# Weighted expert combine on one core: a ring of token slots with one load queue in place of four two-token buffers on two queues

## The chip, the cores and the metric

The kernel runs on one core of a Trainium2 chip. The metric is device time in microseconds (us) of one launch. The kernel before was timed in four runs: 721.25 to 721.85 us, median 721.6 us. One further view of it exists, a profiled execution of 721.47 us, and every duration below comes from that one.

## The reference: what is computed

```python
batch, seq, n_experts, expert_dim = 16, 1024, 8, 512      # all float32
def reference(expert_outputs, combine_weights):
    weights = combine_weights[..., np.newaxis]
    return np.sum(expert_outputs * weights, axis=2).astype(np.float32)
```

For each of 16,384 tokens, eight rows of 512 numbers are multiplied by eight scalars and added up. The input is 268.4 MB, the output 33.6 MB, the weights 0.5 MB. There is no reuse: each input number is read once, multiplied once and added once.

## The kernel before, in words

**Tiling.** 128 partitions each take J = 2 tokens that follow each other, so that one step holds 256 tokens and there are 64 steps. A step's input tile `in_t` is 32 KiB on each partition (4 MiB in all), and the 128 pieces follow each other in memory without a gap. In what follows a "token" is one row of 128 tokens, one on each partition; a step is then two tokens, and the kernel has 128 of them.

**Loads.** `issue_load` (L52 to L62) allots one of four `in_t` buffers and one of four small `w_t` buffers. The 4 MiB load goes to SyncE's queue (SP) for even steps and to ScalarE's (ACT) for odd steps (L56); the last two steps are loaded in two halves (L59). The weights of a step, 8 KiB, are loaded through GpSimd's queue (L60). Three loads are issued ahead; at step n the load of step n+3 is issued, into the buffer that step n-1 has used. So it waits until VectorE has finished step n-1.

**Arithmetic.** For each of the two tokens in turn, VectorE (DVE) writes the product with expert 0 into `acc` (L77, a TENSOR_SCALAR), then seven times adds a product on top (L83, a SCALAR_TENSOR_TENSOR that reads `in_t`, the scalar and `acc`, and writes `acc`). Each of these seven depends on the one before it.

**Stores.** After each step 512 KiB go out (L92), on the queue that did not load that step; each partition's piece is 4 KiB. Loads and stores thus stand behind each other in both queues.

**The last two steps** (L94 on). Experts 4 to 7 of each token are multiplied on ScalarE into bf16 (L111), while VectorE does experts 0 to 3 (L116, L122), sums the products (L130, L135) and adds them (L138). Four stores of 256 KiB on SP end the kernel (L141).

The order of instructions on each queue is that of the program; the framework adds the semaphore waits.

Of the kernel before, what the change touches and what calls it, by code (L numbers as in the profile page):

```python
# [1 line left out]

# [4 lines left out]


@with_exitstack  # L10
def kernel(
    ctx: ExitStack,
    tc: tile.TileContext,
    expert_outputs: bass.AP,
    combine_weights: bass.AP,
    out: bass.AP,
):
    nc = tc.nc
    fp32 = mybir.dt.float32
    bf16 = mybir.dt.bfloat16  # L20

    B, S, E, D = expert_outputs.shape
    T = B * S
    P = 128
    J = 2
    n_steps = T // (P * J)

    eo_blk = expert_outputs.rearrange("b s e d -> (b s) e d").rearrange(
        "(n p j) e d -> n p j e d", p=P, j=J
    )  # L30
    w_blk = combine_weights.rearrange("b s e -> (b s) e").rearrange(
        "(n p j) e -> n p j e", p=P, j=J
    )
    o_blk = out.rearrange("b s d -> (b s) d").rearrange(
        "(n p j) d -> n p j d", p=P, j=J
    )

    in_pool = ctx.enter_context(tc.tile_pool(name="in_pool", bufs=4))
    w_pool = ctx.enter_context(tc.tile_pool(name="w_pool", bufs=4))
    out_pool = ctx.enter_context(tc.tile_pool(name="out_pool", bufs=4))  # L40
    prod_pool = ctx.enter_context(tc.tile_pool(name="prod_pool", bufs=2))

    ES = E // 2
    K_TAIL = 2

    load_engines = [nc.sync, nc.scalar]

    LA = 3
    in_tiles: list[bass.AP | None] = [None] * n_steps
    w_tiles: list[bass.AP | None] = [None] * n_steps  # L50

    def issue_load(m: int) -> None:  # L52
        in_t = in_pool.tile([P, J, E, D], fp32, name="in_t")
        w_t = w_pool.tile([P, J, E], fp32, name="w_t")
        if m < n_steps - K_TAIL:
            load_engines[m % 2].dma_start(out=in_t, in_=eo_blk[m])  # L56
        else:
            for j in range(J):
                load_engines[m % 2].dma_start(out=in_t[:, j], in_=eo_blk[m, :, j])  # L59
        nc.gpsimd.dma_start(out=w_t, in_=w_blk[m])  # L60
        in_tiles[m] = in_t
        w_tiles[m] = w_t  # L62

    for m in range(min(LA, n_steps)):
        issue_load(m)

    for n in range(n_steps):
        if n + LA < n_steps:
            issue_load(n + LA)
        if n >= n_steps - K_TAIL:  # L70
            continue
        in_tile = in_tiles[n]
        w_tile = w_tiles[n]
        acc = out_pool.tile([P, J, D], fp32)

        for j in range(J):
            nc.vector.tensor_scalar_mul(  # L77
                out=acc[:, j, :],
                in0=in_tile[:, j, 0, :],
                scalar1=w_tile[:, j, 0:1],  # L80
            )
            for e in range(1, E):
                nc.vector.scalar_tensor_tensor(  # L83
                    out=acc[:, j, :],
                    in0=in_tile[:, j, e, :],
                    scalar=w_tile[:, j, e : e + 1],
                    in1=acc[:, j, :],
                    op0=mybir.AluOpType.mult,
                    op1=mybir.AluOpType.add,
                )  # L90

        load_engines[(n + 1) % 2].dma_start(out=o_blk[n], in_=acc)  # L92

    tail_steps = list(range(n_steps - K_TAIL, n_steps))  # L94
    tail_accs = {}
    tail_prods = {}
    for n in tail_steps:
        acc = out_pool.tile([P, J, D], fp32, name="acc")
        prods = prod_pool.tile([P, J, E - ES, D], bf16, name="prods")
        tail_accs[n] = acc  # L100
        tail_prods[n] = prods

    for j in range(J):
        for n in tail_steps:
            in_tile = in_tiles[n]
            w_tile = w_tiles[n]
            acc = tail_accs[n]
            prods = tail_prods[n]

            for e in range(ES, E):  # L110
                nc.scalar.mul(  # L111
                    out=prods[:, j, e - ES, :],
                    in_=in_tile[:, j, e, :],
                    mul=w_tile[:, j, e : e + 1],
                )
            nc.vector.tensor_scalar_mul(  # L116
                out=acc[:, j, :],
                in0=in_tile[:, j, 0, :],
                scalar1=w_tile[:, j, 0:1],
            )  # L120
            for e in range(1, ES):
                nc.vector.scalar_tensor_tensor(  # L122
                    out=acc[:, j, :],
                    in0=in_tile[:, j, e, :],
                    scalar=w_tile[:, j, e : e + 1],
                    in1=acc[:, j, :],
                    op0=mybir.AluOpType.mult,
                    op1=mybir.AluOpType.add,
                )
            nc.vector.tensor_add(  # L130
                out=prods[:, j, 0:2, :],
                in0=prods[:, j, 0:2, :],
                in1=prods[:, j, 2:4, :],
            )
            nc.vector.tensor_add(  # L135
                out=prods[:, j, 0, :], in0=prods[:, j, 0, :], in1=prods[:, j, 1, :]
            )
            nc.vector.tensor_add(  # L138
                out=acc[:, j, :], in0=acc[:, j, :], in1=prods[:, j, 0, :]
            )  # L140
            nc.sync.dma_start(out=o_blk[n, :, j], in_=acc[:, j, :])  # L141


# [1 line left out]
_INS = ['expert_outputs', 'combine_weights']  # L145
_OUTS = [((16, 1024, 512), 'float32')]


# [23 lines left out]
```

## Time and profile before

| What | Value |
|---|---|
| median of four runs | 721.6 us |
| the profiled execution | 721.47 us |
| its span in the profile | 719.7 us |
| outside the span | 1.8 us |
| VectorE busy | 644.3 us (90%), 1020 instructions |
| ScalarE busy | 11.4 us, 17 instructions |
| GpSimd busy | 35.6 us, 68 instructions |
| bytes read from and written to memory | 268.96 MB and 33.55 MB |
| first VectorE instruction starts at | 22.86 us |
| last VectorE instruction ends at | 716.08 us |

The span is the stretch from the first to the last recorded event. "Busy" is the union of an engine's instructions; two VectorE instructions that follow each other overlap a little in these records, so that the mean length of one (744 ns for L83) is more than the distance from one start to the next. The DMA rows count the core's 16 DMA engines together: a share of 100% is all 16 moving a packet. The queue of SP is q1, that of ACT is q10, GpSimd's is q0, and q14 fetches instructions.

### The profile page before, as it was taken

To read this page: it belongs to the slowest core of one execution; us is meant where nothing else is said; L and a number is where in the kernel's file an instruction comes from. 1 tells how busy PE (TensorE), PEld (TensorE's weight loads), DVE (VectorE), ACT (ScalarE), POOL (GpSimd) and SP (SyncE) were. 2 spreads that over 40 slices of the span, in tenths; PEclk is the share of its full clock that TensorE was granted. 3 is DMA by queue.
4 is the path that set the end of the run, shared out by engine and by line. 5 is a ranking of instruction groups with operands and counts; after the bars stand their busy time and mean duration, and the time that the engine had idled before them with its cause. 6 is when DMAs were issued, how large, how long until landed. Compare 5 with 4: busy or idle time off the path is not lost.

```text
span 719.7 us, 1532 instructions
## 1 busy us (share of the span) xinstructions
DVE 644.3 (90%) x1020; ACT 11.4 (2%) x17; POOL 35.6 (5%) x68
## 2 busy tenths in 40 slices
DVE  0799999999998999989998999989998999999977
ACT  0000000000000000000000000000000000000023
POOL 1000000000000000000000000000000000000000
DMA  9999999999999999999999999999999999999983
GB/s 380 438 413 446 434 427 430 428 423 428 442 431 441 427 424 427 428 431 438 437 435 426 431 427 428 434 441 431 430 429 427 424 434 439 435 428 429 424 356 138
DMA packets 21068, 302.63 MB, mean 420 GB/s; under 512 B 3136, under 2 KB 4160, under 8 KB 12608
## 3 DMA queue, kind: packets, MB, share of 16 engines
q1 hardware_dynamic: 9792, 151.52, 49.2%
q10 hardware_dynamic: 9216, 150.47, 48.9%
q0 software_dynamic: 2048, 0.53, 0.3%
q14 instruction: 12, 0.10, 0.0%
HBM read 268.96 MB, written 33.55 MB: 420 GB/s over the span
## 4 chain that ended last, share of the span: by engine, by line
DMA 64%; DVE 35%; issue 1%; DVEq 0%; SPq 0%
DMA out_dram<-acc 56%; DVE acc L83 30%; DMA in_t<-in_expert_outputs_dram 8%; DVE acc L77 3%; DVE acc L122 1%; DVE acc L138 0%; DVE prods L130 0%; DVE acc L116 0%; DVE prods L135 0%; DVEq L77 0%; DVEq L116 0%; SPq L92 0%
## 5 line engine op out<-in xcount | busy, mean ns | idle before, releaser
L83 DVE SCALAR_TENSOR_TENSOR acc<-in_t,w_t,acc 128x512 f32<-128x512 f32 x868 | 580.1, 744 | 0.0
L77 DVE TENSOR_SCALAR acc<-in_t,w_t 128x512 f32<-128x512 f32 x124 | 54.6, 482 | 66.2 <-DMA in_t<-in_expert_outputs_dram 43.3
L60 POOL DMA_DIRECT2D w_t<-in_combine_weights_dram x64 | 35.4, 554 | 637.8 <-DVE acc L83 637.0
L111 ACT ACT_TABLE_LOAD x1 | 1.3, 1283 | 690.5 <-DMA in_t<-in_expert_outputs_dram 690.5
L111 ACT ACTIVATE prods<-in_t,w_t 128x512 bf16<-128x512 f32 x16 | 10.1, 710 | 9.2 <-DMA in_t<-in_expert_outputs_dram 9.1
L122 DVE SCALAR_TENSOR_TENSOR acc<-in_t,w_t,acc 128x512 f32<-128x512 f32 x12 | 8.8, 742 | 0.0
L116 DVE TENSOR_SCALAR acc<-in_t,w_t 128x512 f32<-128x512 f32 x4 | 1.9, 479 | 5.5 <-DMA out_dram<-acc 5.5
L138 DVE TENSOR_TENSOR acc<-acc,prods 128x512 f32<-128x512 f32 x4 | 2.7, 684 | 0.0
L130 DVE TENSOR_TENSOR prods<-prods 128x1024 bf16<-128x1024 bf16 x4 | 2.7, 681 | 0.0
L135 DVE TENSOR_TENSOR prods<-prods 128x512 bf16<-128x512 bf16 x4 | 1.7, 413 | 0.0
L156 POOL MEMSET const-float32-0.0<- 128x1 f32 x1 | 0.1, 98 | 0.2 <-issue 0.2
L156 POOL MEMSET const-bfloat16-1.0<- 128x1 bf16 x1 | 0.1, 102 | 0.0
L156 POOL MEMSET const-float32-1.0<- 128x1 f32 x1 | 0.1, 98 | 0.0
L156 POOL MEMSET const-uint8-127<- 128x1 uint8 x1 | 0.1, 98 | 0.0
## 6 DMA issues: line engine op xcount, KB each, us to landing
in_t<-in_expert_outputs_dram ACTq DMA_DIRECT2D x31, 4096.0 KB, 33.5
in_t<-in_expert_outputs_dram SPq DMA_DIRECT2D x31, 4096.0 KB, 33.3
out_dram<-acc ACTq DMA_DIRECT2D x31, 512.0 KB, 33.5
out_dram<-acc SPq DMA_DIRECT2D x31, 512.0 KB, 33.4
in_t<-in_expert_outputs_dram SPq DMA_DIRECT2D x2, 2048.0 KB, 31.2
in_t<-in_expert_outputs_dram ACTq DMA_DIRECT2D x2, 2048.0 KB, 14.0
w_t<-in_combine_weights_dram POOLq DMA_DIRECT2D x64, 8.0 KB, 6.8
out_dram<-acc SPq DMA_DIRECT2D x4, 256.0 KB, 2.6
```

The costliest lines, as they stand in the source:

```text
L60: nc.gpsimd.dma_start(out=w_t, in_=w_blk[m])
L77: nc.vector.tensor_scalar_mul(out=acc[:, j, :], in0=in_tile[:, j, 0, :], scalar1=w_tile[:, j, 0:1],)
L83: nc.vector.scalar_tensor_tensor(out=acc[:, j, :], in0=in_tile[:, j, e, :], scalar=w_tile[:, j, e : e + 1], in1=acc[:, j, :], op0=mybir.Al ...
L111: nc.scalar.mul(out=prods[:, j, e - ES, :], in_=in_tile[:, j, e, :], mul=w_tile[:, j, e : e + 1],)
L116: nc.vector.tensor_scalar_mul(out=acc[:, j, :], in0=in_tile[:, j, 0, :], scalar1=w_tile[:, j, 0:1],)
L122: nc.vector.scalar_tensor_tensor(out=acc[:, j, :], in0=in_tile[:, j, e, :], scalar=w_tile[:, j, e : e + 1], in1=acc[:, j, :], op0=mybir.Al ...
L130: nc.vector.tensor_add(out=prods[:, j, 0:2, :], in0=prods[:, j, 0:2, :], in1=prods[:, j, 2:4, :],)
L135: nc.vector.tensor_add(out=prods[:, j, 0, :], in0=prods[:, j, 0, :], in1=prods[:, j, 1, :])
L138: nc.vector.tensor_add(out=acc[:, j, :], in0=acc[:, j, :], in1=prods[:, j, 0, :])
L156: nc = _bacc.Bacc("TRN2", target_bir_lowering=False, num_devices=1)
```

## The change

The change rewrites the function.

- **Token blocks.** A block is G = 8 tokens that follow each other on each partition, and there are 16 blocks. On one partition a block is 128 KiB of input that lies together, and the next partition's begins 128 KiB further on.
- **Ring.** In place of four two-token buffers there is one tile, `ring`, of ten slots of one token each (16 KiB on a partition). Loads take two slots, 4 MiB, a pair of tokens. The 32 KiB on each partition lie together in memory, and the next partition's 32 KiB are 128 KiB further on; they were adjacent before.
- **One load queue.** All loads go to SP. Four are issued at once, the fifth next; then the load of tokens i+8 and i+9 is issued after VectorE has finished tokens i-2 and i-1, whose slots it takes.
- **Weights.** All weights go into one tile by one DMA on SP ahead of the first load, as 2048 pieces of 256 bytes. The 64 loads through GpSimd's queue are gone.
- **First product.** `first` moves the product with expert 0 to ScalarE, for all 128 tokens. It writes f32 into `acc`, one pair ahead of VectorE.
- **Two chains in turn.** VectorE does experts 1 to 7 of two tokens alternately: token i expert 1, token i+1 expert 1, token i expert 2, and so on. `acc` has sixteen rows, two blocks.
- **Stores.** A block's eight tokens go out in one DMA of 2 MiB on ACT's queue (16 KiB on a partition). The last block goes out as four tokens on ACT, two on SP, and one and one on SP.
- **End.** The last two tokens are loaded in six pieces (experts 0 to 3 and 4 to 7 of token 126; then 3, 2, 2 and 1 experts of token 127). The split between VectorE and ScalarE in the last two steps, and its bf16 products, are gone.
- `PE_TOKENS` is 0, so the branch with TensorE never runs; `make_identity` still fills a tile on GpSimd at the start.

The diff, cut to its core:

```diff
-    in_pool = ctx.enter_context(tc.tile_pool(name="in_pool", bufs=4))
-    load_engines = [nc.sync, nc.scalar]
...
-            load_engines[m % 2].dma_start(out=in_t, in_=eo_blk[m])
...
-        nc.gpsimd.dma_start(out=w_t, in_=w_blk[m])
...
+    x = expert_outputs.rearrange("b s e d -> (b s) e d").rearrange(
+        "(n p g) e d -> n p g e d", p=P, g=G
+    )
+    ring = one.tile([P, SLOTS, E, D], fp32, name="ring")
+    acc = one.tile([P, 2 * G, D], fp32, name="acc")
+    w_t = one.tile([P, T_P, E], fp32, name="w_t")
...
+    loads += [(T_P - 2, 1, 0, 4), (T_P - 2, 1, 4, 8)]
+    loads += [(T_P - 1, 1, 0, 3), (T_P - 1, 1, 3, 5), (T_P - 1, 1, 5, 7), (T_P - 1, 1, 7, 8)]
...
+            if (e0, e1) == (0, E):
+                dst, src = ring[:, s : s + m], x[n, :, g : g + m]
+            else:
+                dst, src = ring[:, s, e0:e1], x[n, :, g, e0:e1]
+            pin(nc.sync.dma_start(out=dst, in_=src))
...
+    def first(i):
+        s, a = i % SLOTS, i % (2 * G)
+            pin(nc.scalar.mul(out=acc[:, a], in_=ring[:, s, 0], mul=w_t[:, i, 0:1]))
...
+    def term(i, e):
+                nc.vector.scalar_tensor_tensor(
+                    out=acc[:, a], in0=ring[:, s, e],
+                    scalar=w_t[:, i, e : e + 1], in1=before, op0=mult, op1=add,
+                )
...
+    pin(nc.sync.dma_start(out=w_t.rearrange("p (n g) e -> p n (g e)", g=G), in_=w))
+    make_identity(nc, ident)
+    load_until(SLOTS - 2)
+    for i in (0, 1):
+        first(i)
+    for i in range(0, T_P, 2):
+        load_until(i + SLOTS)
+        for k in (i + 2, i + 3):
+            if k < T_P:
+                first(k)
+        for e in range(E):
+            for k in (i, i + 1):
+                term(k, e)
+        end = i + 2
+        if end <= T_P - G and end % G == 0:
+            store(end - G, G, nc.scalar)
+        elif end == T_P - 4:
+            store(end - 4, 4, nc.scalar)
+        elif end == T_P - 2:
+            store(end - 2, 2, nc.sync)
+        elif end == T_P:
+            store(end - 2, 1, nc.sync)
+            store(end - 1, 1, nc.sync)
```

## The prediction

> **What bounds the kernel now.** I read the page's table of slices first, then its DMA queues, its groups, and then the trace's table by stretches.
>
> ```profile
> DVE  0799999999998999989998999989998999999977
> DMA  9999999999999999999999999999999999999983
> DMA packets 21068, 302.63 MB, mean 420 GB/s; under 512 B 3136, under 2 KB 4160, under 8 KB 12608
> q1 hardware_dynamic: 9792, 151.52, 49.2%
> q10 hardware_dynamic: 9216, 150.47, 48.9%
> q0 software_dynamic: 2048, 0.53, 0.3%
> ...
> L83 DVE SCALAR_TENSOR_TENSOR acc<-in_t,w_t,acc 128x512 f32<-128x512 f32 x868 | 580.1, 744 | 0.0
> L77 DVE TENSOR_SCALAR acc<-in_t,w_t 128x512 f32<-128x512 f32 x124 | 54.6, 482 | 66.2 <-DMA in_t<-in_expert_outputs_dram 43.3
> ```
>
> Both engines look full. What decides is which of them waits: VectorE's only idle time, 66.2 us ahead of L77, was ended by DMAs (22.9 of it by the first load). The DMA row is full from the start to slice 38, and the three queues make 98.4% of 719.7 = 708.2 us of packet time for each of the 16 engines. VectorE's 644 us lie beneath that.
>
> ```profile
> core 0: us, DVE busy (x) ACT busy (x) POOL busy (x), PEclk, DMA share, GB/s
> 150.00:300.00 150.00, 138.82 (x220) 0.00 (x0) 7.57 (x14) 1.00 1.01 433
> 300.00:450.00 150.00, 137.93 (x218) 0.00 (x0) 6.95 (x13) 1.00 1.00 430
> 450.00:600.00 150.00, 137.03 (x217) 0.00 (x0) 7.49 (x14) 1.00 1.01 432
> ...
> 688.00:692.00 4.00, 4.00 (x8) 1.51 (x2) 0.00 (x0) 1.00 0.68 220
> 693.00:698.00 5.00, 4.37 (x8) 1.33 (x3) 0.00 (x0) 1.00 1.04 444
> 698.00:704.00 6.00, 1.16 (x3) 2.71 (x5) 0.00 (x0) 1.00 0.95 343
> 704.00:708.00 4.00, 4.00 (x8) 2.29 (x4) 0.00 (x0) 1.00 0.59 235
> 708.00:719.70 11.70, 8.05 (x14) 2.56 (x4) 0.00 (x0) 1.00 0.19 73
> ```
>
> Columns: stretch, length, busy time of VectorE, ScalarE and GpSimd with instruction counts, clock, DMA share, GB/s. For 450 us the DMA share is full at 430 to 433 GB/s; only the last 12 us are compute on data that has landed. So time comes off only by less packet time, or by a shorter head or tail.
>
> **Prices of packets.** The trace keeps every packet: 32 KiB takes 1.213 us (the mid value of each queue), 16 KiB 0.611, 8 KiB 0.309, 4 KiB 0.159, 2 KiB 0.086, the weights' 512 B 0.027, a 4-byte semaphore write 0.009. The profile's page bears them out: q10's 3968 loads of 32 KiB, 3968 stores of 4 KiB and 256 loads of 16 KiB, which took 0.705 on the mean, make 5625 us, and 48.9% of 16 x 719.7 is 5631.
>
> **The change, DMA work.** Loads keep their bytes and 32 KiB packets: 268.4 MB are 8192 of them, x 1.213 / 16 = 621.1 us, and 0.2 for the last two tokens' small pieces. Stores: 15 blocks x 128 x 0.611 / 16 = 73.3; four tokens 128 x 0.309 / 16 = 2.5; two 1.3; the last two 1.4; in all 78.5 (before 81.7, since four 4 KiB packets are dearer than one of 16 KiB). Weights: 2048 packets of 256 B, bounded by 0.009 and 0.027, 1.2 to 3.5 us; I take 2.3. Semaphore writes: 89 DMAs x 16 x 0.009 / 16 = 0.8. Sum 702.9 against 708.2: **5.3 us less**.
>
> The Trainium skill (DMA: Bandwidth & Descriptors, Specifications) puts the least size for full rate at 512 bytes, with a read-modify-write below; by it, as an estimate, the 256 B weights cost twice as much, about 2 us more, once. No row here has 256 B packets.
>
> **One load queue.** The added risk is a gap between loads. At 693 to 698 ACT's queue loads nearly alone, in 16 KiB packets, at 444 GB/s: one queue feeds all 16 engines. Depth: after landing, a pair needs ScalarE 0.9 us (L111's 0.71 and a hand-over) and VectorE 9.3, and then its slots reload; three loads, 29 us of work, still stand in SP's queue. That is the cover. If it ran out, each pair would pay up to its 10.2 us. SP holds nothing else until the end: in the built program's order all loads stand on SP as the diff says, each waiting for the pair that leaves its slots, and every earlier DMA that shares a semaphore with it is eight back, landed long before.
>
> **VectorE.** The 128 TENSOR_SCALARs and the tail's 12 sums leave it; 128 x 7 = 896 SCALAR_TENSOR_TENSORs are left, 16 more than before. The spacing is 580.1 / 868 = 0.668 us. Do two chains in turn shorten that? The tail alternates independent work:
>
> ```profile
> 708.51 0.66 DVE acc L122
> 709.17 0.60 DVE prods L130
> 709.77 0.66 DVE acc L122
> ```
>
> L130 does not need L122's result and still starts 0.66 after it. So I price the alternation at nothing (bounds 0.60, the row behind L130, to 0.668). A pair costs 14 x 0.667 = 9.3 us (before 10.2); the DMA needs 8 x 1.213 = 9.7 for its load and 1.2 for its share of stores, 10.9. VectorE waits a little for every pair; its saved time is worth nothing until the end.
>
> **ScalarE and ACT's queue.** 128 products x 0.71 = 91 us, done as each pair lands. A block's store waits on ACT for VectorE's last term; behind it stand the products for the pair after the next, not needed for 9 us. The 2 MiB store has 8 packets on each engine, in turn with loads: 8 x (1.213 + 0.611) = 14.6 us. Its `acc` rows are written again three pairs, 33 us, later: hidden.
>
> **Head.** The weights stand before the first load: about 1 us of issue on top of the 2.3 counted. The first pair lands near 14 us and not 22; that feeds VectorE sooner, which is not the bound. GpSimd's `make_identity` has no reader.
>
> **Tail.** Before, the last load packet ends at 708.0 (packet records), VectorE at 716.08, the span at 719.7. Now the last load lands at 708.0 - 5.3 + 1.0 = 703.7. In front of it lie 9.7 us for tokens 126 and 127, and 2.5 us of the four-token store beside them: tokens 124 and 125 land at 691.5. VectorE then has 28 terms in one run, since the last pair is there before it is reached: 691.5 + 0.9 + 28 x 0.667 = 711.1. The last store and the end take the 3.6 us that they took before: 714.7. With 1.8 us outside the span: **716.5 us**, 5.0 under the profiled 721.47, which is 0.1 under the median of 721.6. The 1.9 us hole before 691 (share 0.68) is not credited: in the packet records one engine, which is late, never has it, and the last landing is that engine's.
>
> **Rivals.**
> *No change (B).* The weights' issue is long. SP and ACT issue 128 pieces in some 0.35 us; if 2048 go in proportion, 5.6 us pass before the first load, 4.6 more than I took: 721.1. For: nothing hides the head of a queue that is full to its end. Against: GpSimd's weight loads hardly show in q0's 0.3%.
> *Slower by row distance (C).* Rows of 32 KiB now lie 128 KiB apart. If this lengthens load packets, all 512 on each engine pay: 10 ns each (0.8%) eat the gain. The nearest row is the slowest full slice, 413 GB/s against 431: at that rate the loads take 621 x 18/413 = 27 us more, 743. Against: all rows now are adjacent, so none shows it, and packets of 1.213 us hardly vary.
>
> The Trainium skill speaks against the change here (DMA: Bandwidth & Descriptors, Latency and other measured facts): copies with a row distance of 512 KiB ran at 207 GB/s where 214 was full, and at 164 with 2 MiB. By the first, as an estimate, loads would take 3.4% or 21 us more, 737; 128 KiB is not in its list, and no run here shows it.
>
> *Slower by store bursts (D).* At 698 to 704 one queue loads while the other stores, and the rate is 343 GB/s at 0.95 share: the 16 KiB load packets stretch, the longest to 1.75 us. If each of 15 bursts ran so, 14.6 x (431/343 - 1) = 3.7 us each, 56 us, 772. It decides from 0.33 us a burst, a tenth of that. Against: in mid-kernel 4 KiB stores of one queue also stand beside loads of the other, at 431.
> *VectorE as the bound* would need 10.9 / 14 = 0.78 us a term; no row is near it.
>
> **How the numbers follow.** My forecast has 0.60. Its own range is 711 (terms at 0.60 us save 1.9, the late engine not late 3.7) to 720 (weights at their upper bound, a head 2 us longer). B has 0.13, C 0.12, D 0.15. About 0.2% (1.4 us) is what a measurement here can tell from none. Faster: 0.60 and 0.02 each from B and from a mild D; same: 0.09 from B, 0.01 from C; slower: 0.02 from B, 0.11 from C, 0.13 from D. The range 710 to 727 holds my case, B, and the mild halves of C and D; about 0.15 lies above it.
>
> **What will show it.** Right: q1 near 88% and q10 near 11% of the span, load packets at 1.213, DMA share near 1.00 from 3 us to 700, L111 of the new file (its term) spaced at 0.667, and 20 to 24 us from the landing of tokens 124 and 125 to the end. Longer load packets everywhere mean C; only beside stores, D; a first load that starts after 5 us, B. Share under 0.97 in mid-kernel would refute the single queue's cover.

## The result, and the profile after

The changed kernel takes 720.5 us (median of 41 runs, 719.9 to 722.2) where the kernel before took 721.5 in the same sessions (61 runs). The ratio is 0.9987, 95% interval 0.9983 to 0.9992. It is faster, by 1.0 us where 5.0 were forecast; that is 0.13%, less than the 0.2% that the forecast took for the least a comparison can tell, and so many runs tell it all the same. The profiled execution's span fell from 719.7 to 718.4 us.

The changed kernel's page, the rows that answer to those of before:

```profile
DVE  0997896978979888898878978789697896978978
DMA  9999999999999999999999999999999999999992
DMA packets 14746, 302.60 MB, mean 421 GB/s; under 512 B 3472, under 2 KB 3472, under 8 KB 4368
q1 hardware_dynamic: 12432, 270.01, 87.6%
q10 hardware_dynamic: 2304, 32.51, 10.6%
...
L111 DVE SCALAR_TENSOR_TENSOR acc<-ring,w_t,acc 128x512 f32<-128x512 f32 x896 | 598.9, 745 | 116.5 <-ACT acc L92 116.5
L92 ACT ACTIVATE acc<-ring,w_t 128x512 f32<-128x512 f32 x128 | 85.5, 714 | 603.4 <-DMA ring<-in_expert_outputs_dram 603.4
```

VectorE's busy time fell from 644 to 599 us and bought nothing, as the DMA row is full to its last slice but one, about as before. The two queues are loads and stores now, 87.6% and 10.6%. Added up packet by packet, without the instruction fetches, the records make 705.6 us for each DMA engine where they made 709.0 before (708.2 by the rounded shares of the page). So the records fell by 3.4, not by 5.3.

The same kernel's table by stretches (stretch, length, busy time of VectorE, ScalarE and GpSimd, clock, DMA share, GB/s):

```profile
core 0: us, DVE busy (x) ACT busy (x) POOL busy (x), PEclk, DMA share, GB/s
150.00:300.00 150.00, 124.28 (x187) 18.19 (x28) 0.00 (x0) 1.00 1.00 433
300.00:450.00 150.00, 129.08 (x194) 17.84 (x27) 0.00 (x0) 1.00 1.00 432
450.00:600.00 150.00, 126.70 (x190) 18.67 (x28) 0.00 (x0) 1.00 1.01 433
...
698.00:704.00 6.00, 6.00 (x10) 0.72 (x1) 0.00 (x0) 1.00 0.67 274
704.00:708.00 4.00, 4.00 (x7) 0.72 (x1) 0.00 (x0) 1.00 0.31 125
708.00:718.40 10.40, 7.39 (x12) 0.00 (x0) 0.00 (x0) 1.00 0.17 63
```

Mid-kernel the rate is 432 to 433 GB/s; before it was 430 to 433. Then look at the end: from 698 on, the share falls to 0.67 and 0.31 although loads are still under way. Of the 16 engines, ten have finished the last load by 700.4 and fifteen by 703.4; the last one finishes it at 708.35 (by the events of the semaphore that the load raises). Its last load packet ends at 707.9 (packet records), where the kernel before had 708.0, so the last landing hardly moved. Before, ScalarE shows it:

```profile
708.48 2.56 ACT L111 ACTIVATE prods<-in_t,w_t 128x512 bf16<-128x512 f32 x4 [2.19 <-DMA in_t<-in_expert_outputs_dram]
```

(Some expectations below put the last landing "near 707"; at 707.1 the last load but one ends.)

The end of the changed kernel in the trace's order of time (start, length, engine, line, operation, tiles, count, and in brackets the idle time before it):

```profile
684.48 1.33 ACT L92 ACTIVATE acc<-ring,w_t 128x512 f32<-128x512 f32 x2 [11.34 <-DMA ring<-in_expert_outputs_dram]
685.24 9.37 DVE L111 SCALAR_TENSOR_TENSOR acc<-ring,w_t,acc 128x512 f32<-128x512 f32 x14 [3.31 <-ACT acc L92]
696.00 0.72 ACT L92 ACTIVATE acc<-ring,w_t 128x512 f32<-128x512 f32 x1 [10.18 <-DMA ring<-in_expert_outputs_dram]
...
696.75 18.64 DVE L111 SCALAR_TENSOR_TENSOR acc<-ring,w_t,acc 128x512 f32<-128x512 f32 x28 [2.15 <-ACT acc L92]
...
705.22 0.72 ACT L92 ACTIVATE acc<-ring,w_t 128x512 f32<-128x512 f32 x1 [6.02 <-DMA ring<-in_expert_outputs_dram]
```

The first row is ScalarE's product when tokens 122 and 123 have landed, the third when token pair 124 and 125 has. VectorE idles 3.3 and 2.15 us ahead of its last two runs, and the last run is the forecast 28 terms, 18.6 us, to 715.4. Its length was right. Its start was not. The last 32 KiB packet of tokens 124 and 125 ends at 695.5 (packet records) and ScalarE starts at 696.0, where the forecast has that landing at 691.5.

### The profile page after: what moved, and what is told of

The parts are those of the page before. It is cut to its first block, busy times and chain, and to the rows that moved or that the text cites. A ratio compares the mean times of both kernels' runs of the same rounds, so it can differ in the third digit from the quotient of the medians.

```text
span 718.4 us, 1327 instructions
## 1 busy us (share of the span) xinstructions
DVE 598.9 (83%) x896; ACT 86.8 (12%) x129; POOL 0.7 (0%) x6
## 3 DMA queue, kind: packets, MB, share of 16 engines
q1 hardware_dynamic: 12432, 270.01, 87.6%
q10 hardware_dynamic: 2304, 32.51, 10.6%
## 4 chain that ended last, share of the span: by engine, by line
DMA 91%; DVE 5%; another core or an unknown queue 1%; ACT 1%; issue 1%; SPq 0%; DVEq 0%; ACTq 0%
DMA ring<-in_expert_outputs_dram 91%; DVE acc L111 5%; ACT acc L92 1%; SPq L83 0%; DVEq L173 0%; SPq L125 0%; ACTq L92 0%; DVEq L111 0%
## 5 line engine op out<-in xcount | busy, mean ns | idle before, releaser
L111 DVE SCALAR_TENSOR_TENSOR acc<-ring,w_t,acc 128x512 f32<-128x512 f32 x896 | 598.9, 745 | 116.5 <-ACT acc L92 116.5
L92 ACT ACTIVATE acc<-ring,w_t 128x512 f32<-128x512 f32 x128 | 85.5, 714 | 603.4 <-DMA ring<-in_expert_outputs_dram 603.4
```

What stands on the lines that cost most here:

```text
L92: pin(nc.scalar.mul(out=acc[:, a], in_=ring[:, s, 0], mul=w_t[:, i, 0:1]))
L111: nc.vector.scalar_tensor_tensor(out=acc[:, a], in0=ring[:, s, e], scalar=w_t[:, i, e : e + 1], in1=before, op0=mult, op1=add,)
```

## The experiments

Each run is compared with the kernel before on its own chip. Where a run is set against the changed kernel, the changed kernel's ratio is 0.9987.

### Stores of one pair, in 4 KiB packets

```diff
-        if end <= T_P - G and end % G == 0:
-            store(end - G, G, nc.scalar)
-        elif end == T_P - 4:
-            store(end - 4, 4, nc.scalar)
+        if end <= T_P - 4:
+            store(end - 2, 2, nc.scalar)
```

> The changed kernel with its 2 MiB stores undone: each pair goes out by itself on ACT's queue, 512 KiB in packets of 4 KiB. Theory A (packet records add up to wall time, as the prediction priced them): 4 packets of 0.159 us in place of one of 0.611, 3.2 us slower than the changed kernel, ratio to the kernel before about 1.003. Theory B (small packets run into the next one, so that much of their price is not seen): at most 1.5 us slower than the changed kernel, ratio at or under 1.001.

Measured: 720.67 us, ratio 0.9989 (0.9980 to 0.9998). The price by records, 3.2 us, isn't there; undoing the large stores costs 0.1 us, with an interval of about 0.7 either way. The DMA view of 150 to 600 us shows why. Three kernels in turn, before, changed, and this one:

```profile
DMA packets 13112, 194.25 MB, mean 432 GB/s; under 512 B 1960, under 2 KB 2605, under 8 KB 7843
q1 hardware_dynamic: 5910, 98.48, 51.0%
q10 hardware_dynamic: 5901, 95.37, 49.4%
```

```profile
DMA packets 7442, 194.56 MB, mean 432 GB/s; under 512 B 816, under 2 KB 816, under 8 KB 816
q1 hardware_dynamic: 5908, 172.10, 88.8%
q10 hardware_dynamic: 1528, 22.41, 11.6%
```

```profile
DMA packets 11846, 194.26 MB, mean 432 GB/s; under 512 B 1318, under 2 KB 1318, under 8 KB 6569
q1 hardware_dynamic: 5926, 172.69, 88.9%
q10 hardware_dynamic: 5913, 21.51, 11.7%
```

In the same 450 us the kernel before moved 194.25 MB, the changed one 194.56 and this one 194.26. The shares of the queues add up to more than 100%: 51.0 + 49.4 with GpSimd's 0.3 is 100.7% before, 88.8 + 11.6 is 100.4% after, 88.9 + 11.7 is 100.6% here. A share above the whole means that records overlap: one packet's record still runs when the next has begun. The packet records show by how much where one engine works alone. At 705 to 707 us of the changed kernel, 4 KiB packets with records of 0.159 us start every 0.155 us; at 704 to 706 us of the run with more fetches (below), 8 KiB packets with records of 0.309 start every 0.306. So a record is 3 to 4 ns longer than the time that its packet takes, at both sizes.

For a pair of tokens each engine stores eight packets of 4 KiB or two of 16 KiB. If every packet overlaps by 4 ns, the six more make 0.024 us, or 1.5 us over 62 pairs. And the load records are shorter in this run, 1.2153 us on the mean against 1.2178, which is 1.3 us for each engine. That leaves some 0.4 of the 3.2.

The distance between landings agrees. Each engine ends its share of a load with a 4-byte write, and these 16 writes are in the packet records. On the middle one of the 16 engines they come 10.96 us apart for each pair before, 10.92 after and 10.93 here: small stores cost about 0.01 us a pair, 0.6 us over the kernel. Theory B holds.

### Weights beside the first loads, not ahead of them

```diff
-    pin(nc.sync.dma_start(out=w_t.rearrange("p (n g) e -> p n (g e)", g=G), in_=w))
+    for n in range(N):
+        nc.gpsimd.dma_start(
+            out=w_t[:, n * G : (n + 1) * G].rearrange("p g e -> p (g e)"), in_=w[:, n]
+        )
```

> The changed kernel with its weights loaded through GpSimd's queue in 16 loads of 32 KiB, beside the first loads and not ahead of them. Theory B (the weights' 2 us at the head are on the path because nothing runs beside them): the first load packet starts near 1.8 us and not at 3.7, and the kernel ends 1 to 2 us sooner, ratio 0.996 to 0.9975. Rival A (the weights' packets cost the same wherever they stand): within 0.5 us of the changed kernel, ratio 0.998 to 0.9995.

Measured: 720.69 us, ratio 0.9987 (0.9979 to 0.9996). My theory B fell and A held. The first load packet does start at 1.7 us and not at 3.7, but the first four loads then land 10.3 to 10.4 us apart and not 9.7, as the weights' packets stand among theirs. By 680 us the changed kernel has moved 291.99 MB and this one 292.10 (packet records up to that time), which differ by 0.2 us of work. The weights cost the same 2 us of DMA wherever they are put, and the head is no loss of its own.

### More instruction fetches

```diff
+        if i < 112:
+            for _ in range(8):
+                pin(nc.vector.memset(tiny, 0.0))
```

> The changed kernel with 448 tiny VectorE instructions added in its idle time (eight one-element writes behind each of the first 56 pairs; VectorE idles 116 us in the changed kernel). They add 3 to 4 instruction fetches of 8 KiB. Theory L (one DMA engine carries the fetches, falls behind, and its landing sets the end): 0.7 to 1 us each, 2.5 to 3.5 us slower than the changed kernel, ratio 1.002 to 1.0035, and the last engine's landings later by as much. Rival (lateness of one engine has another cause, or does not set the end): under 0.6 us, ratio under 0.9997.

Measured: 724.54 us, ratio 1.0040 (1.0027 to 1.0054), 4.0 us slower than the changed kernel. The queue of instruction fetches has 13 packets of 8 KiB in this span where the changed kernel's has 10; the changed kernel's tenth comes at 710 us, behind the last load, so 13 stand against 9. Its table by stretches at the end:

```profile
core 0: us, DVE busy (x) ACT busy (x) POOL busy (x), PEclk, DMA share, GB/s
700.00:704.00 4.00, 2.84 (x5) 2.06 (x3) 0.00 (x0) 1.00 0.72 297
704.00:708.00 4.00, 4.00 (x7) 0.00 (x0) 0.00 (x0) 1.00 0.06 27
708.00:712.00 4.00, 4.00 (x7) 0.72 (x1) 0.00 (x0) 1.00 0.21 85
```

0.06 is one engine out of sixteen. At 704 to 708 fifteen DMA engines have finished everything and one is still loading. The end in order of time:

```profile
700.40 0.72 ACT L93 ACTIVATE acc<-ring,w_t 128x512 f32<-128x512 f32 x1 [10.30 <-DMA ring<-in_expert_outputs_dram]
...
701.16 18.64 DVE L112 SCALAR_TENSOR_TENSOR acc<-ring,w_t,acc 128x512 f32<-128x512 f32 x28 [2.27 <-ACT acc L93]
```

Tokens 124 and 125 land at 700.4 where they landed at 696.0; VectorE's last run is as long as before and still has 2.3 us of idle time ahead of it. So VectorE's added work did not delay it, the landing did. In the packet records a fetch takes 0.31 to 0.33 us, and the load packet that starts right behind it takes 1.59 to 1.875 us and not 1.213.

The records don't name engines, but the 16 completion writes of each load say how far the slowest engine is behind the middle one (us, at loads with no large store beside them):

| Near | 130 us | 250 us | 360 us | 490 us | 610 us | 666 us |
|---|---|---|---|---|---|---|
| kernel before | 0.7 | 2.4 | 3.1 | 4.9 | 5.6 | 6.4 |
| changed kernel | 0.8 | 2.5 | 3.2 | 4.1 | 5.1 | 6.1 |
| this run | 1.5 | 3.5 | 5.4 | 7.0 | 8.8 | 8.7 |

In the changed kernel the second-slowest engine is never more than 1 us behind the middle at these loads. The lag of the slowest grows in steps, and each step stands right behind a fetch: 0.9 to 1.0 us behind those at 247, 336, 435, 524 and 622 us in the changed kernel, 0.8 to 1.0 behind those at 161, 227, 284, 349, 415, 471, 538 and 593 in this run. In each of the two kernels two fetches (279 and 368; 280 and 371) add no step. So one engine carries most of the fetches. Theory L stands, at about 1 us a fetch: four fetches more, 4.0 us.

### Experts 0 to 4 of the last two tokens on TensorE

```diff
-    PE_TOKENS = 0
-    PE_EXPERTS = 3
+    PE_TOKENS = 2
+    PE_EXPERTS = 5
```

> The changed kernel with the dormant branch switched on for the last two tokens: TensorE multiplies experts 0 to 4 by diagonal matrices that ScalarE makes and adds them in PSUM, VectorE adds the last three. VectorE's run after the landing of tokens 124 and 125 falls from 28 terms to 20. Theory T (that run sets the end): 3 to 5 us sooner than the changed kernel, ratio 0.9915 to 0.9945; not the full 5.3 us, since the last load lands near 707 us and a term, a store and the end follow it. Rival P (TensorE's products, f32 and on a cold clock, come later than VectorE needs them): no gain or a loss, ratio 0.998 or more.

Measured: 718.91 us, ratio 0.9962 (0.9949 to 0.9975), 1.8 us sooner than the changed kernel; 3 to 5 were expected. The end in order of time:

```profile
698.05 9.37 DVE L111 SCALAR_TENSOR_TENSOR acc<-ring,w_t,acc 128x512 f32<-128x512 f32 x14 [2.22 <-ACT acc L92]
...
699.92 11.30 PE L98 MATMUL ps<-ring,diag 128*128 128x512 f32 x20 [699.92 <-ACT diag L97]
...
707.33 0.74 DVE L111 SCALAR_TENSOR_TENSOR acc<-ring,w_t,ps 128x512 f32<-128x512 f32 x1
...
711.26 0.75 DVE L111 SCALAR_TENSOR_TENSOR acc<-ring,w_t,ps 128x512 f32<-128x512 f32 x1 [3.19 <-PE ps L98]
711.93 2.73 DVE L111 SCALAR_TENSOR_TENSOR acc<-ring,w_t,acc 128x512 f32<-128x512 f32 x4
```

VectorE's last run is now 14 terms and then six, and within the six, behind the first, it waits 3.2 us for TensorE (the bracket of the last but one row): TensorE's ten products take 11.3 us from 699.9 on. Part of theory T, part of P.

### Three experts on TensorE

```diff
-    PE_TOKENS = 0
+    PE_TOKENS = 2
```

> The changed kernel with the dormant branch on for the last two tokens as it stands, three experts on TensorE: VectorE's last run falls from 28 terms to 24. Theory T (this run sets the end): 2.7 us less, so 1.5 to 2.7 us sooner than the changed kernel, ratio 0.995 to 0.9965; TensorE's six products need 6 to 7 us, less than the eleven of the ten before, so VectorE waits under 1 us for them where it waited 3.2. Rival P (the last landing and TensorE behind it set the end already): no better than with five experts on TensorE, ratio 0.996 or more.

Measured: 720.83 us, ratio 0.9985 (0.9975 to 0.9995), runs from 718.9 to 722.0. The expectation missed: no gain can be told in the median. In the profiled execution, 719.86 us, VectorE waited 1.35 us for TensorE and ended at 715.07, only 0.3 sooner than in the changed kernel. Its tokens 124 and 125 also landed later there, at 696.9 and not 696.0; why isn't known.

### One engine left out of one load

```diff
+            if i == 100:
+                for p0, p1 in ((0, 120), (120, 128)):
+                    pin(nc.sync.dma_start(out=ring[p0:p1, s : s + m], in_=x[n, p0:p1, g : g + m]))
+                loaded += 1
+                continue
```

> The changed kernel with one load, that of tokens 100 and 101, cut into one of 120 partitions and one of 8. The number of DMA engines that share a load goes with its partitions: the first can use 15, the second 8, so that one engine gets no part of this pair (9.7 us of packets less) and eight get one packet more (1.2 us). Theory L (one engine, late by its instruction fetches, some 8 us at the end, sets the landings), if the late engine is the one left out: landings of the last pairs 5 to 8 us sooner, end 4 to 6.5 us sooner than the changed kernel, ratio 0.9895 to 0.993. If the late engine is another: 0 to 1.5 us slower than the changed kernel, ratio 0.9985 to 1.001. Rival (no engine is late for long, all land together): within 0.5 us of the changed kernel.

Measured: 736.76 us, ratio 1.0203 (1.0186 to 1.0220). All three expectations missed. Queue q1 has seven completion writes more than in the changed kernel (packet records), as 15 and 8 engines for the two parts make. The table by stretches shows what came instead:

```profile
500.00:560.00 60.00, 44.05 (x67) 6.43 (x10) 0.00 (x0) 1.00 1.01 387
560.00:570.00 10.00, 9.02 (x14) 0.24 (x1) 0.00 (x0) 1.00 1.07 234
570.00:580.00 10.00, 0.00 (x0) 0.00 (x0) 0.00 (x0) 1.00 0.94 338
...
600.00:620.00 20.00, 16.29 (x26) 2.67 (x4) 0.00 (x0) 1.00 1.00 430
```

The share is 1.07 and 0.94 at 234 and 338 GB/s: the engines are occupied and move far less. It begins at 540 us: up to there the rate is 432 GB/s, then 300 and 292 in the two stretches of 10 us ahead of these rows. Load packets last up to 4.9 us there, and the rate is back at 430 behind 600. Cutting this load by partitions costs far more than the late engine does. Why the packets grow so long is not shown, and which engine is late stays open.

### The cut load and three experts on TensorE together

> Both edits together: the load of tokens 100 and 101 in 120 and 8 partitions, and three experts of the last two tokens on TensorE. If the late engine is the one left out and VectorE's last run sets the end, the gains add up: 5.5 to 9 us sooner than the changed kernel, ratio 0.986 to 0.991. If only TensorE's part works: as that run by itself, 0.995 to 0.998.

Measured: 737.73 us, ratio 1.0225 (1.0193 to 1.0257). The cut load decides it, as in the run before.

### Loads on two queues

```diff
-            pin(nc.sync.dma_start(out=dst, in_=src))
+            q = nc.sync if (i // 2) % 2 == 0 or i >= 108 else nc.scalar
+            pin(q.dma_start(out=dst, in_=src))
```

> The changed kernel with its loads on SP and ACT in turn up to token 107, as the kernel before has them, and the rest as changed. Theory Q (with all loads on one queue an instruction fetch lengthens the late engine's next load packet by 0.4 to 0.66 us, where on two it was mostly 0.1 to 0.2): packets behind a fetch shorten again and the last landing comes 1 to 3 us sooner, ratio 0.9945 to 0.9975. Rival (the number of queues is indifferent): within 0.6 us of the changed kernel, ratio 0.998 to 0.9995.

Measured: 721.17 us, ratio 0.9993 (0.9982 to 1.0004), runs from 719.7 to 722.9. Theory Q fell: load packets behind a fetch still take up to 1.875 us. The time by itself says little about one queue against two, because this kernel has another end:

```profile
669.75 47.78 DVE L112 SCALAR_TENSOR_TENSOR acc<-ring,w_t,acc 128x512 f32<-128x512 f32 x72
```

VectorE runs 72 terms, 47.8 us, without a pause, so it is behind at the end. The trace's table of waits puts 125.6 us of ScalarE's waits ahead of its products down to stores, up to 13.3 us at once, and VectorE waited up to 36.6 us for a product. That the loads and stores on ScalarE's own queue cause this is argued, not shown.

### The changed kernel again, halves, and halves with sequence

The first edit halves the loads of tokens 120 to 125 by experts; the second sums the last two tokens one after the other.

```diff
-    for t in range(BULK, T_P - 2, 2):
+    for t in range(BULK, T_P - 8, 2):
         loads += [(t, 2, 0, E)]
+    for t in range(T_P - 8, T_P - 2, 2):
+        loads += [(t, 2, 0, 4), (t, 2, 4, 8)]
...
-                dst, src = ring[:, s, e0:e1], x[n, :, g, e0:e1]
+                dst, src = ring[:, s : s + m, e0:e1], x[n, :, g : g + m, e0:e1]
...
-        for e in range(E):
-            for k in (i, i + 1):
-                term(k, e)
+        if i == T_P - 2:
+            order = [(k, e) for k in (i, i + 1) for e in range(E)]
+        else:
+            order = [(k, e) for e in range(E) for k in (i, i + 1)]
+        for k, e in order:
+            term(k, e)
```

> The changed kernel as it is, for the comparison with the two that follow on the same chip: 0.9975 to 0.9995 of the kernel before.

Measured: 720.54 us, ratio 0.9987 (0.9978 to 0.9995).

> The halves alone, with the last two tokens in turn. Theory T: VectorE starts the last two tokens sooner, but its second term belongs to token 127, whose first piece lands near 705 us, so it stalls some 4 us there and 12 or 13 terms, 8 us, follow: at most 2 us sooner than the changed kernel, ratio to the kernel before 0.996 to 0.9985. Rival: no different from the run with both edits.

Halves alone: 720.82 us, ratio 0.9991 (0.9982 to 1.0000). No gain that is clear of noise; VectorE stalls 3.25 us for token 127 and 13 terms follow, as theory T has it.

> The changed kernel with two edits at the end: the loads of tokens 120 to 125 come in halves of four experts, so that VectorE can begin a pair when its first half has landed; and the last two tokens are summed one after the other, not in turn, so that token 126 does not wait for token 127's load. Theory T (the end is set by VectorE's run of 28 terms behind the landing of tokens 124 and 125, and 5.5 us of its idle time ahead of that run can be used): VectorE ends 3.5 to 5 us sooner, close behind the last landing near 707 us, ratio to the changed kernel 0.993 to 0.9955, to the kernel before 0.9915 to 0.9945. Rival (the last landing on the late engine sets the end whatever VectorE does, or more and smaller loads cost as much as they give): within 1 us of the changed kernel.

Both edits: 718.78 us, ratio 0.9961 (0.9948 to 0.9973), 1.8 us under the changed kernel beside it. Halves with sequence, in order of time:

```profile
686.45 5.39 DVE L113 SCALAR_TENSOR_TENSOR acc<-ring,w_t,acc 128x512 f32<-128x512 f32 x8 [1.38 <-DMA ring<-in_expert_outputs_dram]
...
692.11 4.07 DVE L113 SCALAR_TENSOR_TENSOR acc<-ring,w_t,acc 128x512 f32<-128x512 f32 x6 [0.27 <-ACT acc L94]
697.02 16.16 DVE L113 SCALAR_TENSOR_TENSOR acc<-ring,w_t,acc 128x512 f32<-128x512 f32 x22 [0.85 <-DMA ring<-in_expert_outputs_dram]
...
705.55 0.72 ACT L94 ACTIVATE acc<-ring,w_t 128x512 f32<-128x512 f32 x1 [3.60 <-DMA ring<-in_expert_outputs_dram]
```

VectorE starts tokens 124 and 125 at 692.1 and not 696.75, waits 0.85 us for their second half, and from 697.0 has 22 terms and not 28: it ends at 713.2 in place of 715.4. The direction is theory T's, the size half of it: VectorE was bound by the second half's landing, 1 us later than the pair landed in the changed kernel. The sequence without the halves was not run, so what the halves add to it is not shown.

### Halves, sequence and TensorE together

> Both working tail edits together: halves and sequence, and experts 0 to 4 of the last two tokens on TensorE. VectorE's run behind the landing of tokens 124 and 125 falls from 22 terms to 14. If the edits add up (the tail is VectorE's): VectorE ends 1.5 to 3 us sooner than with halves and sequence alone, ratio to the kernel before 0.992 to 0.9945. If the last landing, now at 709 us, with TensorE's products behind it sets the end: within 1 us of halves and sequence alone, 0.995 to 0.997.

Measured: 720.63 us, ratio 0.9990 (0.9981 to 0.9999). The gains did not add up, they went:

```profile
701.85 11.40 PE L100 MATMUL ps<-ring,diag 128*128 128x512 f32 x20 [701.85 <-DMA ring<-in_expert_outputs_dram]
...
709.00 0.75 DVE L113 SCALAR_TENSOR_TENSOR acc<-ring,w_t,ps 128x512 f32<-128x512 f32 x1 [6.07 <-PE ps L100]
...
713.29 0.75 DVE L113 SCALAR_TENSOR_TENSOR acc<-ring,w_t,ps 128x512 f32<-128x512 f32 x1 [1.97 <-PE ps L100]
```

TensorE starts when the load that it waits for has landed, at 701.85 (the first bracket), where it started at 699.92 with the whole loads. VectorE waits 6.1 us for its sum of token 126, then 2.0 for that of token 127, which is there when TensorE's 11.4 us are over. The two best versions are thus five experts on TensorE alone (0.9962) and halves with sequence (0.9961), and nothing run here has both gains.

## Why the prediction was right or wrong

**Right.** The bound: DMA packets, not VectorE. One queue fed all 16 engines, at a share of 1.00 to 1.01. Load packets stayed at 1.213 us in the mid value (mean 1.218, before 1.215), so rival C fell; the trace shows no loss at a row distance of 128 KiB, which the Trainium skill's list (DMA: Bandwidth & Descriptors, Latency and other measured facts) doesn't have. Rival D fell: the rate is 432 to 433 GB/s over stretches that hold ten of the large stores. The weights' 256-byte packets took 0.018 us each, 2.3 us in all as I took, and not twice that. Rival B fell: the weights' DMA was issued in 0.43 us. The alternation of chains was worth nothing: 598.9 / 896 = 0.668 us a term, the number of before. The end was VectorE's 28 terms behind the landing of tokens 124 and 125.

**Wrong.** The step that failed is the sum of DMA work, "Sum 702.9 against 708.2: 5.3 us less". Two parts of that saving did not exist as time.

- *Unlike sums.* 708.2 is a total of records as they were, with their long packets in it; 702.9 is made of mid values. At the same mid values the packets of before make 706.3 (loads 621.2, stores 81.6, weights 1.7, semaphore writes 1.8). So 1.9 of the 5.3 were never a saving: the load records make 624 us in both kernels, where I had 621.3 for the changed one.
- *The stores, 78.5 against 81.7.* I added records of packets of different sizes as if they stood end to end. The run with 4 KiB stores shows this term at 0.1 us in the time and at 0.6 in the distance of the landings, where I had 3.2.

The last landing was to come 4.3 us sooner (5.3 less 1.0 of head). It came 0.1 sooner: 707.9 where it had been 708.0. Of the 4.3, the unlike sums take 1.9 and the stores 2.6. The head gave 1.3 back: the first load starts at 3.7 us, and I had counted 1.74 + 2.3 + 1.0 = 5.0. That makes 1.1 sooner. The completion writes say much the same: 0.042 us less for each of 62 pairs is 2.6, the first load starts 1.9 later, and the slowest engine's lag is 0.3 less, which makes 1.0. The rest, 1 us, was lost at the end. A likely place, not tested: in the kernel before, eleven 4 KiB store packets of the late engine, 1.7 us, still stood behind the last load packet, and in the changed kernel the stores up to token 123 are done ahead of it.

The instruction fetches are no part of the miss. The late engine was 6.4 us behind the middle one before and is 6.1 behind it now, though the load packets behind fetches lengthened more: before, part of that fell on the 4 KiB store packets.

The rest of the tail was sized rightly. I had 12.2 us from the landing of tokens 124 and 125 to the last; 12.4 were measured (last packets at 695.5 and 707.9). So these tokens landed 4.0 late. From there to VectorE's start it took 1.25 us and not 0.9, the 28 terms took 18.6 as I had it, and VectorE ends at 715.4 where I had 711.1. The end behind it took 3.0 and not 3.6, which by luck hides 0.6 of the miss.

That the late engine's hole at 691 was not credited was right. The other engines gained it, and fifteen had finished the last load by 703.4; the end does not see them.

The Trainium skill (DMA: Bandwidth & Descriptors, Latency and other measured facts) says that engines 7 and 15 are usually slower, and guesses that the rings of GpSimd's DMAs cause it. The changed kernel issues no DMA from GpSimd, and one engine ends 8 us behind the middle one all the same; here the lateness goes with instruction fetches. Which engine it is, no run here shows.

## What to carry to other kernels

Where DMA bounds a kernel, don't add packet records as wall time: queue shares above 100% say that records overlap. Bytes moved in a fixed stretch, or the distance from one landing to the next, are the better measure. And compare like sums: a total of records with a total, mid values with mid values. A transfer has landed when its slowest engine has, so look at the end for a DMA share that falls in steps towards one sixteenth while loads are still open; work that is taken off the other fifteen is not seen. In such a kernel the last microseconds are bought by what the compute engine still has to do behind the last landings.

## What was not expected of the hardware

- One of 16 DMA engines finishes the last load 8 us after the middle one and 5 after the next, and more instructions on VectorE make it later: 448 more brought four more fetches and cost 4.0 us, though VectorE had idle time for all of them.
- A load cut into 120 and 8 partitions made the DMA run at 234 to 338 GB/s with a full share for 40 us, and cost 16 us in all.
- 512 KiB of weights cost 2 us of DMA time both as one DMA ahead of everything and as 16 beside the loads.
